# Later rotations and splits of q and k, side-by-side starts of the mixers' output products, and head transposes among the gates' products, in a four-layer block kernel

## The chip, the cores and the metric

The kernel runs on one core of one Trainium2 chip. The metric is device time in microseconds (us), the median of several executions; lower is better. Engines are called PE (TensorE, matmuls), ACT (ScalarE), DVE (VectorE), POOL (GpSimd) and SP (SyncE, which issues the DMAs).

## The reference

Two blocks of two layers each work on 256 latent tokens and 256 context tokens of 1024 features, in f32. Each layer is a mixer followed by an mlp (1024 to 4096 to 1024, squared relu); norms before both are modulated by numbers that come from a vector `c` through a matrix `w_mod` of 1024 x 6144. The first block's mixer has three branches, pooling, a gating unit and neighbourhood attention; its latent q and k are rotated. The second block's mixers are an mLSTM (both directions) and a windowed attention (SWA).

```python
def first_block(...):
    ...
        p, u, vs, q, k, v, gl = jnp.split(a @ w_in[l], SPLIT_POINTS, axis=-1)
        attn = neighbourhood_attention(apply_rope(to_heads(q), cos, sin), apply_rope(to_heads(k), cos, sin),
                                       to_heads(v), k_ctx, v_ctx, na_rpb[l], rows)
        mix = merge_branches(pool_mix(p, w_pool[l], pool_scale[l]), sgu_mix(u, vs, sgu_w[l], sgu_b[l]),
                             attn.reshape(h.shape[0], n_lat, NA_WIDTH), gl,
                             w_pool_out[l], w_sgu_out[l], w_attn_out[l], w_o[l])
        h = h + g1 * mix
        h = h + g2 * sq_relu_mlp(modulate(rms_norm(h, norm2_g[l]), sh2, sc2), w_ff1[l], w_ff2[l])
def merge_branches(pool_o, sgu_o, attn_o, gate_logits, w_po, w_so, w_ao, w_o):
    gp, gs, ga = jnp.split(jax.nn.sigmoid(gate_logits), N_BRANCH, axis=-1)
    y = gp * (pool_o @ w_po) + gs * (sgu_o @ w_so) + ga * (attn_o @ w_ao)
    return y @ w_o
```

In the mLSTM each head's result is normed over its 128 features, scaled by `head_norm`, multiplied by the sigmoid of an output gate (a product of the normed input) and then by `w_out`. In the SWA sixteen query heads share four key heads; latent q and k are rotated.

## The kernel before, in words

Features lie on the partitions, tokens along the free axis: 512 columns, context first (0 to 255), latents after (256 to 511). Every f32 operand is split into a high and a low f32r part. A large product goes by column tiles of 128 outputs (`gemm`, L204): a weight tile of 128 x 1024 comes by DMA into `raw`, ACT writes its high part `whi`, DVE (or POOL) the low part `wlo`, and for each of the eight row tiles PE issues three matmuls (high x high, high x low, low x high) into one PSUM bank. `raw`, `whi` and `wlo` have three slots each. A tile with both streams is 24 matmuls of 512 columns. With `head=n` the first n column tiles run side by side, one stream after the other (256 columns, SKEW row tiles apart), with `tail=n` the last n.

`evac` functions take a product up. They may return a part that `flush` issues when the next product's matmuls are under way (`take`, L196; `flush`, L233). `evac_k` (L813) and `evac_q` (L824) serve the first block's attention: they copy the latent half from PSUM to a T1 tile, split the context half straight from PSUM (`put_k`, L707; `put_q`, L714: ACT the high parts, DVE the low ones), rotate (`rope`, L687: a matmul with `perm`, a POOL and two DVE instructions) and split the rotated half. `gemm_rows` (L263) computes values with tokens on the partitions, four PSUM banks side by side, named by a list of tags. PSUM tags are mm (2 banks), mx, S (2), T (2) and acc. SBUF tags have fixed slots: A and B 16 each for the operands of large products in turn, Q 12, E 2, W 3, T1 9, G 2.

Modulation of later layers is worked off in pieces that `drip` (L470) issues after column tiles at a layer's rate (`RATES`); a piece is a DMA, an ACT scaling, a DVE accumulation and a POOL sum into `macc`. After a group of pieces PE sums over partitions (`acc`), ACT copies the sums (`mod_out`, L410), PE transposes them and DVE adds a bias; the transposition is put off by one flush. `need` (L481) issues all pending pieces that a use requires.

The attention output `evac_a` (L976, inside the loop over `wao`) gates a tile on DVE, adds the other branches on POOL (L979) and splits it. `gates_out` (L1229) computes the mLSTM's eight gate tiles; after them all, eight heads are transposed by PE into S banks, gated and split. The engines run their queues in order; a list scheduler orders each queue when the program is built, by priorities that follow the program order (`sooner`, L107, moves the taking up of a product ahead).

## Time and profile before

| | |
|---|---|
| median of 3 runs | 2331.84 us (2328.53 to 2334.13) |
| span of the profiled execution (no other time of it is given) | 2329.3 us |
| PE busy | 2228.5 us, 96% |
| DVE busy | 1620.0 us, 70% |
| ACT busy | 1148.6 us, 49% |
| POOL busy | 681.5 us, 29% |
| mean granted PE clock | 0.981 of full speed |

The span runs from the first to the last instruction. Busy shares are means over stages; a wait is read from the timeline of the engine that stood, where the bracket behind a row gives its idle time and what ended it. The granted clock is 1.00 at 2.4 GHz and 0.50 at 1.2 GHz. A line number can be that of a helper (L116 is `act`, L119 `stt`, L122 `mm`, L126 `tr`, L130 `split`), so tiles by tag say more. T stands for T1 tiles in SBUF and for the PSUM tag T.

### The profile page before, as it was taken

What the parts mean: (1) busy time and instruction counts of PE and PEld (TensorE: products, weight loads), DVE (VectorE), ACT (ScalarE), POOL (GpSimd) and SP (SyncE); (2) the same over time, 40 slices, a digit from 0 to 9 for tenths busy, and PEclk for the clock granted to TensorE, in tenths of its full rate; (3) what the DMA queues carried; (4) which work ended last, traced back from release to release, by engine and by line L of the source; (5) the groups of instructions that cost most, each with busy time, mean ns of one, the idle gap of its engine ahead of it and who ended that gap; (6) DMA issues with size and microseconds to landing.
All of it is one profiled execution on the core that took longest, in us unless ns stands there. A gap on an engine that the chain in (4) does not pass through costs nothing.

```text
span 2329.3 us, 36255 instructions
## 1 busy us (share of the span) xinstructions
PE 2228.5 (96%) x13402; PEld 1864.1 (80%) x13402; DVE 1620.0 (70%) x2762; ACT 1148.6 (49%) x2122; POOL 681.5 (29%) x530
## 2 busy tenths in 40 slices
PE   6899999999999999999999899999999999998998
PEld 3776777787777787798899867778777778768998
DVE  4876656677666885778877755678776566687766
ACT  3455434454443455655544645555443433665453
POOL 1540434524221542045300504154432222423001
PEclk9999999999999999999999999999999999999999
DMA  7351345445655443366554313254555532214552
GB/s 271 128 156 61 124 148 167 133 136 179 193 190 167 144 151 110 113 209 209 190 185 149 114 55 104 86 165 134 157 189 182 167 119 72 82 37 136 191 184 98
DMA packets 128145, 336.78 MB, mean 145 GB/s; under 512 B 14944, under 2 KB 24160, under 8 KB 127968
## 3 DMA queue, kind: packets, MB, share of 16 engines
q1 hardware_dynamic: 127968, 334.46, 44.5%
q8 instruction: 106, 1.74, 0.3%
q14 instruction: 71, 0.58, 0.1%
HBM read 333.36 MB, written 1.05 MB: 144 GB/s over the span
## 4 chain that ended last, share of the span: by engine, by line
PE 47%; DVE 6%; issue 2%; ACT 2%; POOL 2%; DMA 1%; DVEq 0%; POOLq 0%; SPq 0%; ACTq 0%
PE mm L122 27%; PE mx L122 11%; PE S L122 3%; PE num L122 2%; PE T L122 1%; PE pv L122 1%; PE T L126 1%; DVE wlo L130 1%; DMA mraw<-wmod_in 1%; DVE T L119 1%; DVE macc L119 1%; ACT whi L116 1%; POOL macc L449 1%; DVE A L119 1%; DVE B L119 0%
## 5 line engine op out<-in xcount | busy, mean ns | idle before, releaser
L122 PE MATMUL mm<-A,whi 128*128 128x256 f32 (+1 forms) x2600 | 666.2, 344 | 17.5 <-ACT A L116 7.6
L449 POOL TENSOR_TENSOR macc<-macc,mraw 128x512 f32<-128x512 f32 x244 | 363.3, 1489 | 697.0 <-ACT mraw L116 688.6
L122 PEld LDWEIGHTS mm<-A,whi 128*128 128x128 f32 x2600 | 446.7, 191 | 88.5 <-issue 18.8
L122 PE MATMUL mm<-B,whi 128*128 128x256 f32 (+1 forms) x1884 | 456.8, 333 | 8.4 <-DVE T L659 4.2
L122 PE MATMUL mm<-A,wlo 128*128 128x256 f32 (+1 forms) x1300 | 442.0, 340 | 0.0
L130 DVE TENSOR_TENSOR wlo<-raw,whi 128x1024 fp32r<-128x1024 f32 x252 | 344.7, 1370 | 136.4 <-ACT whi L116 134.8
L116 ACT ACTIVATE whi<-raw 128x1024 fp32r<-128x1024 f32 x273 | 287.6, 1055 | 280.7 <-PE mm L122 164.7
L122 PEld LDWEIGHTS mm<-B,whi 128*128 128x128 f32 x1884 | 319.2, 190 | 49.6 <-issue 11.1
L122 PE MATMUL mx<-A,whi 128*128 128x512 f32 (+1 forms) x1256 | 321.1, 343 | 1.6 <-ACT G L116 1.0
L116 ACT ACTIVATE mraw<-mraw,silu 128x512 f32<-128x512 f32 x244 | 175.2, 722 | 290.7 <-DVE macc L119 180.4
L122 PE MATMUL mm<-B,wlo 128*128 128x256 f32 (+1 forms) x942 | 312.1, 332 | 1.6 <-DVE wlo L130 1.6
L119 DVE SCALAR_TENSOR_TENSOR macc<-mraw,silu,macc 128x512 f32<-128x512 f32 x244 | 255.2, 1046 | 58.7 <-DMA mraw<-wmod_in 56.6
L122 PEld LDWEIGHTS mm<-A,wlo 128*128 128x128 f32 x1300 | 248.3, 191 | 28.4 <-issue 2.1
L116 ACT ACTIVATE whi<-Y 128x1024 fp32r<-128x1024 f32 x152 | 160.8, 1058 | 217.5 <-PE mm L122 145.8
L130 DVE TENSOR_TENSOR wlo<-Y,whi 128x1024 fp32r<-128x1024 f32 x148 | 192.4, 1300 | 92.2 <-ACT whi L116 92.0
L122 PEld LDWEIGHTS mx<-A,whi 128*128 128x128 f32 x1256 | 216.4, 190 | 32.0 <-issue 2.5
L122 PE MATMUL mx<-A,wlo 128*128 128x512 f32 (+1 forms) x628 | 214.9, 342 | 0.3 <-DVE wlo L130 0.3
L122 PE MATMUL mx<-B,whi 128*128 128x256 f32 (+1 forms) x836 | 201.4, 329 | 6.6 <-ACT B L116 3.3
L122 PEld LDWEIGHTS mm<-B,wlo 128*128 128x128 f32 x942 | 179.2, 190 | 21.0 <-issue 2.0
L509 POOL TENSOR_TENSOR sums<-sums,T 128x256 f32<-128x256 f32 x84 | 91.3, 1097 | 301.7 <-ACT T L116 300.2
L119 DVE SCALAR_TENSOR_TENSOR h<-mm,mod,h 128x256 f32<-128x256 f32 x278 | 125.8, 478 | 71.6 <-PE mm L122 71.3
L122 PEld LDWEIGHTS mx<-B,whi 128*128 128x128 f32 x836 | 140.9, 191 | 24.3 <-ACT B L116 3.9
(302 smaller groups left out, 3076.4 us busy)
## 6 DMA issues: line engine op xcount, KB each, us to landing
mraw<-wmod_in SPq DMA_DIRECT2D x352, 256.0 KB, 2.9
Y<-ff_in SPq DMA_DIRECT2D x152, 512.0 KB, 4.0
raw<-ff_in SPq DMA_DIRECT2D x104, 512.0 KB, 3.7
raw<-win_in SPq DMA_DIRECT2D x68, 512.0 KB, 3.6
raw<-mwin_in SPq DMA_DIRECT2D x17, 512.0 KB, 3.5
raw<-wo_in SPq DMA_DIRECT2D x16, 512.0 KB, 4.2
raw<-swin_in SPq DMA_DIRECT2D x10, 512.0 KB, 3.4
B<-wfirst_in SPq DMA_DIRECT2D x16, 256.0 KB, 5.4
```

Of the source, the lines that this page charges most:

```text
L116: return self.nc.scalar.activation(out, in_, func, **kw)
L119: return self.nc.vector.scalar_tensor_tensor(out, a, scalar, b, op0, op1)
L122: return self.nc.tensor.matmul(out, lhsT=lhsT, rhs=rhs, start=start, stop=stop, **kw)
L126: return self.nc.tensor.transpose(out, in_, self.ident[:k, :k])
L130: (eng or self.nc.vector).tensor_sub(lo, src, hi.bitcast(F32))
L449: self.nc.gpsimd.tensor_add(a1, a1, raw)
L509: (adder or self.nc.gpsimd).tensor_add(sums, sums, sq)
```

## The change

Eight parts. (1) The ACT copy of modulation sums is issued at once, their transposition two flushes later instead of one. (2) `evac_k` of the first block copies the whole PSUM bank once to an E tile; both halves are split in the put-off part. (3) `evac_q` copies the bank once to a W tile; rotation and splits are put off, with a flush after each `weigh`. (4) In `evac_a` DVE adds instead of POOL for the last two tiles. (5) The three output products `wo0`, `wo1` and `mwout` start with `head=3`; after such tiles there is no `drip`. (6) The mLSTM's and the SWA's `gemm_rows` use the S banks first. (7) Each mLSTM head's transposes, gating and split are put off behind the next gate product. (8) In the SWA k and q are copied once, rotated and split in put-off parts. The diff also strips comments and docstrings, which are left out below.

```diff
-            self.late.append(self.mod_out(i, (cg,), 4 * half, ps))
+            columns = self.mod_out(i, (cg,), 4 * half, ps)
+            self.late.append(lambda: self.late.append(columns))
...
-        self.flush()
+        while self.late:
+            self.flush()
...
     def evac_k(j, ps, a, e):
-        t = b.T1()
-        b.act(t, ps[:, L:])
-        b.put_k(kh[j], kl[j], slice(0, L), ps[:, :L])
+        t = b.t("E")
+        b.act(t, ps)
 
         def rest():
             k = b.T1()
-            b.rope(k, t, b.perm1, b.rope1)
+            b.rope(k, t[:, L:], b.perm1, b.rope1)
+            b.put_k(kh[j], kl[j], slice(0, L), t[:, :L])
             b.put_k(kh[j], kl[j], slice(L, T), k)
         return rest
 
     def evac_q(j, ps, a, e):
-        q, t, k = b.t("Y", (P, 2, T), F32R), b.T1(), b.T1()
-        b.act(t, ps[:, L - a:], scale=0.125)
-        if c0 == 0:
-            b.put_q(q, slice(0, L), ps[:, :L], 0.125)
-        b.rope(k, t, b.perm1, b.rope1)
-        b.put_q(q, slice(L, T), k)
+        q, t = b.t("Y", (P, 2, T), F32R), b.t("W")
+        b.act(t[:, a:], ps, scale=0.125)
         qs.append(q)
 
+        def rest():
+            k = b.T1()
+            b.rope(k, t[:, L:], b.perm1, b.rope1)
+            if c0 == 0:
+                b.put_q(q, slice(0, L), t[:, :L])
+            b.put_q(q, slice(L, T), k)
+        return rest
...
-    b.gemm([win[6 + j] for j in range(4)], xs, c0, evac_q)
+    b.gemm([win[6 + j] for j in range(4)], xs, c0, evac_q, flush=False)
...
             b.weigh(o, qt, pts, vt, vcols)
+            b.flush()
...
-            nc.gpsimd.tensor_add(t, t, y[d][:, c0:])
+            (nc.vector if d > 5 else nc.gpsimd).tensor_add(t, t, y[d][:, c0:])
...
-        b.gemm(aps, ys, c0, b.add_to_h(g1), tail=3, mid=b.norm(xs, LAT, A, S))
+        b.gemm(aps, ys, c0, b.add_to_h(g1), head=3, tail=3, mid=b.norm(xs, LAT, A, S))
...
-        b.gemm(aps, ys, c0, b.add_to_h(g1, then=scale), tail=3)
+        b.gemm(aps, ys, c0, b.add_to_h(g1, then=scale), head=3, tail=3)
...
-        b.gemm_rows([io["mwv"][hf, j] for j in range(4)], T, xs, ("mm", "mm", "S", "S"),
+        b.gemm_rows([io["mwv"][hf, j] for j in range(4)], T, xs, ("S", "S", "mm", "mm"),
...
-    def gates_out():
-        go = [b.t("B") for _ in range(8)]
-        b.gemm([win[16 + j] for j in range(8)], xs, 0,
-               lambda j, ps, a, e: b.act(go[j][:, a:e], ps, AF.Tanh, scale=0.5))
-        return go
+    def gates_out(hs):
+        ys = b.new_xs("A")
+        def evac(hd, ps, a, e):
+            go = b.t("B")
+            b.act(go, ps, AF.Tanh, scale=0.5)
+            def rest():
+                pt = b.ps("S")
+                for c in range(4):
+                    b.tr(pt[:, c * P:(c + 1) * P], hs[hd // 4][c][:, hd % 4, :])
+                t = b.t("E")
+                b.stt(t, go, 1.0, pt, ALU.add, ALU.mult)
+                b.act(ys[hd][0], t, scale=hn[:, hd:hd + 1])
+                b.stt(ys[hd][1], t, hn[:, hd:hd + 1], ys[hd][0].bitcast(F32),
+                      ALU.mult, ALU.subtract)
+            return rest
+        b.gemm([win[16 + j] for j in range(8)], xs, 0, evac)
+        return ys
 
     prj = project(0)
     hs = [heads(0, prj[0], prj[1], prj[3], states(0, prj[2], prj[3]))]
     prj = project(1)
     hs.append(heads(1, prj[0], prj[1], prj[3], states(1, prj[2], prj[3])))
-    go = gates_out()
-    ys = b.new_xs("A")
-    for hd in range(8):
-        pt = b.ps("S")
-        for c in range(4):
-            b.tr(pt[:, c * P:(c + 1) * P], hs[hd // 4][c][:, hd % 4, :])
-        t = b.t("E")
-        b.stt(t, go[hd], 1.0, pt, ALU.add, ALU.mult)
-        b.act(ys[hd][0], t, scale=hn[:, hd:hd + 1])
-        b.stt(ys[hd][1], t, hn[:, hd:hd + 1], ys[hd][0].bitcast(F32), ALU.mult, ALU.subtract)
+    ys = gates_out(hs)
...
-    b.gemm([io["mwout"][d] for d in range(8)], ys, 0, b.add_to_h(b.mod[i][:, 2]), tail=3,
+    b.gemm([io["mwout"][d] for d in range(8)], ys, 0, b.add_to_h(b.mod[i][:, 2]), head=3, tail=3,
            mid=b.norm(xs, LAT, A, S))
...
     def evac_k(j, ps, a, e):
-        if a < L:
-            b.put_k(kh[2 * j:2 * j + 2], kl[j], slice(0, L), ps[:, :L - a])
-        if e > L:
-            t, k = b.T1(), b.T1()
-            b.act(t, ps[:, max(L - a, 0):])
-
-            def rest():
+        t = b.T1()
+        b.act(t, ps)
+
+        def rest():
+            k = t
+            if a == L:
+                k = b.T1()
                 b.rope(k, t, perm2, rope2)
-                b.put_k(kh[2 * j:2 * j + 2], kl[j], slice(L, T), k)
-            return rest
-
-    def query(ps):
-        t, q = b.T1(), b.T1()
+            b.put_k(kh[2 * j:2 * j + 2], kl[j], slice(a, e), k)
+        return rest
+
+    def query(_, ps, a, e):
+        t, out = b.T1(), b.t("Q", (P, 2, L), F32R)
         b.act(t, ps, scale=0.125)
-        b.rope(q, t, perm2, rope2)
-        out = b.t("Q", (P, 2, L), F32R)
-        b.put_q(out, slice(0, L), q)
-        return out
+        qs.append(out)
+
+        def rest():
+            q = b.T1()
+            b.rope(q, t, perm2, rope2)
+            b.put_q(out, slice(0, L), q)
+        return rest
 
     b.gemm([win[8 + j] for j in range(2)], xs, 0, evac_k, head=2, pre=pre, flush=False)
-    b.gemm_rows([io["swv"][j] for j in range(2)], L, xs, ("mm", "mm", "mx", "S"),
+    b.gemm_rows([io["swv"][j] for j in range(2)], L, xs, ("S", "S", "mm", "mm"),
                 lambda c, ps: b.act(vt[c], ps))
     at = []
     qs = []
 
     def project(t):
-        b.gemm([win[t]], xs, L, lambda _, ps, a, e: qs.append(query(ps)))
+        b.gemm([win[t]], xs, L, query, flush=False)
...
             b.weigh(o, qt, pts, vt, vcols)
+            b.flush()
```

Three places in the order, names without their tile counters. First PE in the q products of the first mixer (`mm_1214`, `mx_1280` or `mx_1264`, `mm_1323` are banks of q tiles, `T_...<-...,perm` the rotation of the first q tile). Before:

```order
L122 MATMUL mm_1214<-A_113,wlo_1211 128x512
L122 MATMUL acc_1263<-macc,sel 32x128 x8
L122 MATMUL mx_1280<-A_99,whi_1276 128x512
L122 MATMUL mx_1280<-A_100,whi_1276 128x512
L122 MATMUL mx_1280<-A_99,wlo_1277 128x512
L122 MATMUL T_1247<-T_259_1240,perm_119_490 128x256
L122 MATMUL mx_1280<-A_101,whi_1276 128x512
```

Now:

```order
L122 MATMUL mx_1264<-A_113,whi_1260 128x512
L122 MATMUL mx_1264<-A_114,whi_1260 128x512
L122 MATMUL mx_1264<-A_113,wlo_1261 128x512
L122 MATMUL T_1290<-W_1240,perm_119_490 128x256
L122 MATMUL mm_1323<-A_99,whi_1319 128x512
L122 MATMUL mm_1323<-A_100,whi_1319 128x512
```

The rotation of the first q tile stood behind three matmuls of the second q tile; now it stands behind all 24.

Second, DVE at the start of the first mixer's output product (`G_3331`, `G_3332` are the last two gated tiles, `B_2937`, `B_2939` the low parts of row tiles 6 and 7 of its operand, `wlo_3538`/`wlo_3504` the second column tile's low weights, `wlo_3582`/`wlo_3510` the third's). Before:

```order
L130 TENSOR_TENSOR wlo_3538<-raw_3535,whi_3537 128x1024
L119 SCALAR_TENSOR_TENSOR macc<-mraw_3574,silu_71,macc 128x512
L119 SCALAR_TENSOR_TENSOR G_3331<-G_3331,mm_3431 128x512
L119 SCALAR_TENSOR_TENSOR macc<-mraw_3618,silu_71,macc 128x512
L130 TENSOR_TENSOR B_2937<-G_3331,B_2936 128x512
L119 SCALAR_TENSOR_TENSOR G_3332<-G_3332,mm_3448 128x512
L130 TENSOR_TENSOR wlo_3582<-raw_3579,whi_3581 128x1024
L130 TENSOR_TENSOR B_2939<-G_3332,B_2938 128x512
```

Now:

```order
L130 TENSOR_TENSOR wlo_3504<-raw_3501,whi_3503 128x1024
L119 SCALAR_TENSOR_TENSOR macc<-mraw_3766,silu_71,macc 128x512
L119 SCALAR_TENSOR_TENSOR G_3331<-G_3331,mm_3431 128x512
L119 SCALAR_TENSOR_TENSOR macc<-mraw_4005,silu_71,macc 128x512
L986 TENSOR_TENSOR G_3331<-G_3331,Y_2089 128x512
L119 SCALAR_TENSOR_TENSOR G_3332<-G_3332,mm_3448 128x512
L130 TENSOR_TENSOR B_2937<-G_3331,B_2936 128x512
L986 TENSOR_TENSOR G_3332<-G_3332,Y_2089 128x512
L130 TENSOR_TENSOR wlo_3510<-raw_3507,whi_3509 128x1024
L130 TENSOR_TENSOR B_2939<-G_3332,B_2938 128x512
```

The two sums (L986) stand on DVE, ahead of the third column tile's low weights, which on PE are now wanted 24 matmuls of 256 columns after the product's start; before, the third tile's were wanted after two whole tiles. On ACT the third tile's high part (`whi_3509`) stands between the splits of row tiles 6 and 7.

Third, PE at the values of the mLSTM's first half (`mm_13147` and `mm_13195` are the last q tile; the four banks of the values follow; every group is six matmuls). Before:

```order
L122 MATMUL mm_13147<-A_12547,wlo_13144 128x512
L122 MATMUL mm_13182<-whi_13188,A_12533 128x512
...
L122 MATMUL S_13184<-whi_13188,A_12533 128x512
...
L122 MATMUL mm_13183<-whi_13188,A_12533 128x512
...
L122 MATMUL S_13184<-whi_13188,A_12535 128x512
...
L122 MATMUL S_13185<-whi_13188,A_12533 128x512
```

Now:

```order
L122 MATMUL mm_13195<-A_12589,wlo_13192 128x512
L126 MATMUL T_13230<-ident_118,T_2559_13187 128x128
L122 MATMUL S_13237<-whi_13243,A_12575 128x512
...
L122 MATMUL S_13238<-whi_13243,A_12575 128x512
...
L122 MATMUL mm_13239<-whi_13243,A_12575 128x512
...
L122 MATMUL mm_13240<-whi_13243,A_12575 128x512
```

Both S banks come first, then the mm bank that the q tile before last has left, and last the one of the last q tile, `mm_13240`, which before was `mm_13183`, wanted after nine matmuls.

## Rows read from the trace of the kernel before

**Rows 1.** The page: busy us (share of the span) xinstructions.

```profile
PE 2228.5 (96%) x13402; PEld 1864.1 (80%) x13402; DVE 1620.0 (70%) x2762; ACT 1148.6 (49%) x2122; POOL 681.5 (29%) x530
```

**Rows 2.** Windows behind two waits: PE, PEld, DVE, ACT, POOL busy, PEclk, DMA, GB/s.

```profile
112.00:115.00 3.00, 3.00 (x9) 2.32 (x9) 3.00 (x3) 1.67 (x2) 1.44 (x1) 0.50 0.02 7
...
1345.00:1348.00 3.00, 3.00 (x8) 2.32 (x8) 2.31 (x6) 1.96 (x6) 0.00 (x0) 0.51 0.52 173
```

**Rows 3.** Timeline of PE (start us, us, what, xcount, [idle before <-releaser]), first mixer's third k tile.

```profile
111.66 0.47 PE L126 MATMUL T<-ident,T 128*128 128x128 f32 x1 [5.13 <-ACT T L116]
```

**Rows 4.** Timeline of ACT, the same place.

```profile
108.94 1.28 ACT L116 ACTIVATE Q<-T 64x256 fp32r<-64x256 f32 x3 [2.51 <-DVE T L694]
...
111.33 0.28 ACT L116 ACTIVATE T<-acc 128x128 f32<-128x128 f32 x1
```

**Rows 5.** Windows, columns as in rows 2: two stretches by VectorE's load.

```profile
100.00:125.00 25.00, 19.72 (x76) 15.32 (x77) 22.38 (x30) 14.75 (x30) 12.85 (x10) 0.86 0.27 91
...
1075.00:1100.00 25.00, 20.88 (x156) 20.30 (x155) 22.98 (x25) 14.02 (x25) 17.51 (x13) 0.91 0.72 225
```

**Rows 6.** Timeline of PE, the q tiles of the first mixer.

```profile
153.62 0.70 PE L122 MATMUL T<-T,perm 128*128 128x256 f32 x2 [2.17 <-ACT T L116]
162.45 0.70 PE L122 MATMUL T<-T,perm 128*128 128x256 f32 x2 [1.87 <-ACT T L116]
```

**Rows 7.** Timeline of PE without waits: 512 columns, then 256 columns.

```profile
103.88 0.39 PE L122 MATMUL mm<-A,wlo 128*128 128x512 f32 x1
104.11 0.40 PE L122 MATMUL mm<-A,whi 128*128 128x512 f32 x1
...
2003.01 0.28 PE L122 MATMUL mm<-B,wlo 128*128 128x256 f32 x1
2003.13 0.40 PE L122 MATMUL mm<-B,whi 128*128 128x256 f32 x2
```

**Rows 8.** Timeline of PE, second layer, start of the values.

```profile
896.68 0.47 PE L122 MATMUL mx<-whi,A 128*128 128x512 f32 x1 [3.24 <-DVE Q L712]
```

**Rows 9.** Timelines of PE and POOL, first mixer's output product.

```profile
406.17 0.63 PE L122 MATMUL mx<-B,whi 128*128 128x512 f32 x2
...
415.09 0.51 PE L122 MATMUL mx<-B,whi 128*128 128x512 f32 x1 [3.26 <-ACT B L116]
412.13 2.25 POOL L979 TENSOR_TENSOR G<-G,Y 128x512 f32<-128x512 f32 x1
```

**Rows 10.** Timelines of PE and ACT, mLSTM, first half's values.

```profile
1344.11 0.50 PE L122 MATMUL mm<-whi,A 128*128 128x512 f32 x1 [2.86 <-ACT Q L116]
1342.95 0.63 ACT L116 ACTIVATE nM<-W 64x512 fp32r<-64x512 f32 x1 [2.92 <-DVE W L1061]
```

**Rows 11.** What PE waited for (us in total, times, longest): 1525 to 1550, then 2000 to 2100.

```profile
PE mm L122 <- DVE A L119: 1.2, 2, 0.7
PE mm L122 <- ACT A L116: 0.5, 1, 0.5
...
PE S L122 <- ACT E L116: 1.9, 3, 1.4
PE S L122 <- DVE Q L119: 1.6, 1, 1.6
```

**Rows 12.** The page's groups: busy, mean ns of one, idle before.

```profile
L449 POOL TENSOR_TENSOR macc<-macc,mraw 128x512 f32<-128x512 f32 x244 | 363.3, 1489 | 697.0 <-ACT mraw L116 688.6
L119 DVE SCALAR_TENSOR_TENSOR macc<-mraw,silu,macc 128x512 f32<-128x512 f32 x244 | 255.2, 1046 | 58.7 <-DMA mraw<-wmod_in 56.6
```

**Rows 13.** Line 712 by tile: ns min/median/max, first and last start us.

```profile
L712 DVE TENSOR_TENSOR Q<-T,Q x20: 406/422/1469, 98.0 to 1992.0; 64x256 fp32r<-64x256 f32 x20
L712 DVE TENSOR_TENSOR Q<-mm,Q x12: 404/418/429, 92.9 to 1988.2; 64x256 fp32r<-64x256 f32 x12
```

**Rows 14.** What PE waited for, 1060 to 1120.

```profile
PE mm L122 <- DVE T L659: 4.2, 1, 4.2
PE T L122 <- POOL sums L509: 2.6, 1, 2.6
```

## The prediction

> **What bounds the kernel now.** I read the share of the span first [rows 1]: TensorE is busy for 2228.5 of 2329.3 us, VectorE for 1620.0, ScalarE for 1148.6. So TensorE sets the end, and a change that adds matmuls rather than removing them can win only out of the 100.8 us in which TensorE stands. The list of what it waited for, stretch by stretch, shows that these are single waits of 1 to 5 us, each at a hand-over from a product to ScalarE or VectorE. Third, the table of windows shows what a wait costs beside itself: five of the waits looked at here are followed by 3 us or more at the lower level of the granted clock (1.2 of 2.4 GHz; 0.50 and 0.51 in the first and the last of the five) [rows 2], with TensorE busy all the time; at half speed 3 us of work are 1.5 us lost. The timelines of PE, ACT, DVE and POOL around each wait then name the late instruction. The sum below is made against the profiled execution's span, 2329.3 us; the median of the three runs is 2331.84, and the 2.5 us between them are taken to stay.
>
> **The change part by part.**
>
> *Modulation transposes, first mixer.* TensorE stands 5.13 us at 111.66 for a transposition that waits for a ScalarE copy [rows 3]. That copy ran at 111.33, behind copies of k of which the first had waited 2.51 us for VectorE [rows 4]. Now it stands ahead of those and its transposition one product later. At most 5.1 + 1.5 (clock) = 6.6 us go. But VectorE is busy for 22.38 of 25 us here [rows 5]; the low parts of the next weights come from it in order, and a product without waits would soon reach weights that are not ready. What is late next is a wlo. Bounds 0 and 6.6; I take 2.5, nearer to the lower end since 90% of that stretch is VectorE's.
>
> *Rotations of q, first mixer.* The rotation matmul stands three matmuls into the next product and waits 2.17 and 1.87 us for a ScalarE copy [rows 6]. In the new order it stands behind all 24 matmuls of that product, 24 x 0.23 = 5.5 us later (0.23 from the starts of 512-column matmuls) [rows 7]. Both waits go, and with the second one a half-clock stretch: 2.17 + 1.87 + 1.5 = 5.5. Between 0 and 5.5 I take 5, as the cover is over twice the wait. The bank of the product itself is now read by one copy instead of several.
>
> *k in the second layer.* The product of values stands 3.24 us for a bank whose last reader is a subtraction on VectorE that followed a rotation's sum and two of ScalarE's copies [rows 8]. One ScalarE copy now frees it, and the low parts come from the copy. 3.24 + 1.5 for the clock = 4.7, between none and that; the copy is one instruction that waits for the product alone, so I take 4.5.
>
> *Output product, first mixer.* TensorE stands 3.26 us for the last row tile of its operand: ScalarE's split waited for a GpSimd sum of 2.25 us queued behind two modulation sums [rows 9]. Now VectorE adds the last two, and the first three column tiles run side by side, so that the last row tile is wanted later. Removed: 3.3 + 1.5 = 4.8. But the third tile's weights are now wanted 24 matmuls of 256 columns, 24 x 0.12 = 2.9 us [rows 7], after the start at 406.17 [rows 9], so at 409.1. Their slot is free only after the product that ends there. In the new order the way to them then is a gating, a modulation sum, the sum, the split of row tile 6 and the high part; at about 1 us for each (1.05 for the modulation sum of the same 512 columns [rows 12]) the high part is there at 411.2 and the low part, 1 us more, at 412.2: an estimated new wait of 3 us. I take a gain of 2, between none and 4.8.
>
> *Values of the mLSTM.* TensorE waits 2.86 us until 1344.11 for a bank that ScalarE has to copy out, because ScalarE's queue stood for 2.92 us on a VectorE scan ahead of that copy [rows 10]. The scan and that order stay. Nine matmuls had run, so the product began at 1344.11 - 2.86 - 9 x 0.23 = 1339.2. Now twelve matmuls into two S banks and six into a free one come first: 1339.2 + 18 x 0.23 = 1343.3, which leaves 0.8 us of wait. Gain 2.0, and 1.5 if the clock then stays up: between 1 and 3.5, I take 3.
>
> *Heads' transposes among the gates' products.* TensorE waited 1.2 + 0.5 = 1.7 us for the operand in 1525 to 1550 [rows 11]. The operand's slots (tag A, 16) are those of the gates' own operand, so the splits still can't be written before the last gate product has read them; only transposes and the first gatings move forward. I take 1.5, with 0 and 1.7 as the bounds.
>
> *SWA.* Its waits are 1.9 + 1.6 us in 2000 to 2100 [rows 11]. Rotation and split of q(t+1) now come after the weighing of tile t, so that only the next project product lies between them and the scores that need them, while ScalarE and VectorE are busy with softmax there. A gain of 2, bounds -3 (a loss, as much as is now waited) and 3.5.
>
> *What is added.* Six column tiles (three here, three of the mLSTM) are issued as 48 matmuls of 256 instead of 24 of 512: 24 x (2 x 0.12 - 0.23) = 0.24 us each, 1.4 in all. The second layer's output product was 256 wide already. Skipping the drip for three tiles moves 3 x 1.4, 3 x 0.7 and 3 x 1.4 modulation pieces, ten in all, into the mlp that follows; a piece is 1.05 us of VectorE and 1.49 of GpSimd [rows 12]. Most lie beside products that have time for them; I charge 1.6 us. DMAs of these pieces move along with them, their number stays.
>
> The subtractions of k's context half read SBUF twice now, not PSUM and SBUF. There are 20 of them (4 tiles, 2 halves, 2 layers, and 4 in the SWA). In the trace those that read PSUM last 404 to 429 ns, and those that read SBUF twice have nearly the same median, 422, but reach 1469 [rows 13]. If each of the 20 were stretched so, VectorE would have 20 x 1.05 = 21 us more; the median says most are not, and I charge nothing. The Trainium skill has a rule that speaks against this step: "GPSIMD Engine Reference", section Specifications, says that GpSimd shares its SBUF interfaces with VectorE and contends with VectorE instructions that have two SBUF inputs. The rows agree as to which group has the long ones; by the rule alone the subtractions next to GpSimd's rotations would all be long, and the sum would be nearer to the second rival below.
>
> Sum: -2.5 - 5 - 4.5 - 2 - 3 - 1.5 - 2 + 1.4 + 1.6 = **-17.5 us**, so a span of 2311.8 and a median of **2314 us**.
>
> **The rivals.**
>
> *Everything pays.* All waits named go with their half clocks: 6.6 + 5.5 + 4.7 + 4.8 + 3.5 + 1.7 + 3.5 = 30.3, less the 1.4 of split matmuls: 2303. For it: these waits are single hand-overs, with products on either side of each. Against it: the 22.38 of 25 us, and the third weights.
>
> *VectorE takes over.* Where TensorE no longer waits for a hand-over it waits for low parts of weights. Then the first, fourth, sixth and seventh parts give nothing, the q part half, the mLSTM part 1.5, and the added 3.0 stay: -2.5 - 4.5 - 1.5 + 3.0 = -5.5, 2326. For it: VectorE's 22.38 of 25 us at 100 and 22.98 of 25 at 1075 [rows 5]; against it: 70% over the span.
>
> *Slower: modulation pieces displaced into the norms.* The ten pieces come due around the norm at the mlp's start. There TensorE already stands 4.2 us for VectorE's modulated norm and 2.6 for GpSimd's sums of squares in 1086 to 1120 [rows 14]. Were each piece in line with the norm, it would delay it by 1.05 + 1.49 = 2.5 us, 25 in all and 23 more than charged: 2314 + 23 = 2337. It decides against the change from about eight pieces in line. Against it: TensorE works on context tiles beside most of a norm, and after the first and third mixer the pieces are spread at 2.0 and 1.8 a tile.
>
> *It doesn't do what it says.* The order rows show the moves in place, so this gets no chance of its own.
>
> **How the numbers follow.** Forecast 0.52, everything pays 0.14, VectorE takes over 0.20, slower 0.14. About 0.2%, 4.7 us, is what a measurement of this kernel can tell from no change: below 2327.2 counts as faster, above 2336.5 as slower. The second rival lies at that lower edge and is split, 0.09 faster and 0.11 same. Faster 0.52 + 0.14 + 0.09 = 0.75, same 0.11, slower 0.14. The forecast's own range is 2306 to 2323 (its unknown bounds); for 8 in 10 it reaches down to 2299, 4 us past the case in which everything pays, and up to 2334, which takes in the second rival and leaves out the slower one.
>
> **What would show it.** Right: no T wait on ACT T at the second k tile and at the q tiles of the first mixer; no wait for DVE Q before the second layer's values; the stretches behind them at full clock; a first wait of about 3 us on whi or wlo in the first output product; under 1 us at the mLSTM's values. Wrong: waits on wlo in the stretch after 112 that add up to what went; waits for DVE T or POOL sums at the mlp starts of over 10 us more; SWA longer than its part now. If the half-clock stretches stay though the waits go, the five terms of 1.5 fall out and the gain is up to 7 us smaller.

## The result, and the profile after

The change made the kernel slower: 2350.75 us (median, 2347.44 to 2358.72) beside 2330.48 of the kernel before on the same chip, ratio 1.0091 with a 95% interval of 1.007 to 1.0112. Forecast were 2314 us and a range of 2299 to 2334. The profiled execution has a span of 2345.5 us where before had 2329.3, 16.2 more. The page of the kernel after, busy times as in [rows 1]:

```profile
PE 2239.2 (95%) x13546; PEld 1880.7 (80%) x13546; DVE 1610.4 (69%) x2766; ACT 1156.7 (49%) x2124; POOL 658.3 (28%) x526
```

TensorE has 144 matmuls more, as forecast (six tiles of 48 instead of 24), and is busy for 10.7 us more, of which these explain 1.4; the mean granted clock is 0.975 where before had 0.981. So only 5.5 of the 16.2 us are more standing (106.3 us for 100.8): most of the loss is the same work taking longer, as it did in the half-clock stretches behind waits [rows 2]. No other engine is closer to full than before. What TensorE waits for, the places of [rows 3], [rows 6], [rows 8 to 10] and of the SWA tell in the timeline of PE in the kernel after (the bracket is the wait before the row):

```profile
113.83 0.67 PE L122 MATMUL T<-E,perm 128*128 128x256 f32 x2 [3.73 <-DVE T L695]
...
172.18 1.52 PE L122 MATMUL S<-Q,Y 128*128 128x512 f32 x2 [6.81 <-ACT E L116]
...
411.39 0.51 PE L122 MATMUL mm<-B,whi 128*128 128x256 f32 x2 [1.94 <-ACT whi L116]
...
413.19 0.39 PE L122 MATMUL mm<-B,wlo 128*128 128x256 f32 x1 [1.18 <-DVE wlo L130]
...
895.47 0.50 PE L122 MATMUL mx<-whi,A 128*128 128x512 f32 x1 [2.33 <-ACT E L116]
...
1338.55 0.50 PE L122 MATMUL mm<-whi,A 128*128 128x512 f32 x1 [0.57 <-ACT Q L116]
...
2019.86 2.24 PE L122 MATMUL S<-Q,Q 128*128 128x512 f32 x3 [3.13 <-DVE Q L119]
```

Each named wait is gone or shorter, but most have a successor: 5.13 us for ScalarE's copy became 3.73 for VectorE's half of a rotation; the two waits of 2.17 and 1.87 at the q tiles became one of 6.81 for a softmax; 3.24 at the values became 2.33; the SWA's 1.6 for VectorE's split became 3.13, while its 1.9 for ScalarE [rows 11] is gone. Only the mLSTM's values went as hoped, from 2.86 to 0.57. And one place is new, the norm at the start of the mLSTM's mlp:

```profile
1594.69 0.39 PE L122 MATMUL mm<-B,wlo 128*128 128x256 f32 x1 [2.58 <-DVE wlo L130]
...
1603.29 0.65 PE L122 MATMUL acc<-macc,sel 128*32 128x128 f32 x8 [4.38 <-DVE macc L119]
1605.73 0.65 PE L122 MATMUL acc<-macc,sel 128*32 128x128 f32 x8 [1.79 <-POOL macc L449]
...
1607.05 0.43 PE L122 MATMUL T<-mean,sums 128*128 128x1 f32 x2
...
1610.24 1.22 PE L122 MATMUL T<-ident,sm 128*128 128x128 f32 x4 [1.49 <-POOL sm L524]
1613.00 0.58 PE L122 MATMUL mx<-B,whi 128*128 128x256 f32 x1 [1.54 <-ACT B L116]
```

There TensorE waits for the last modulation sums (`acc<-macc`), and the norm's own first product (`T<-mean,sums`) stands behind them.

To see the stages apart I take marks that every version has: the `T<-mean,sums` that begins a norm (a: first layer's mlp, b: second layer's mixer, c: mLSTM's mixer, f: mLSTM's mlp, g: SWA; of two streams the second, in c the first) and the first `kv` product of each half of the mLSTM (d, e). The table has their starts in the timeline of PE, as the kernel's own minus before's; h is the span. Before: a 463.99, b 842.97, c 1279.58, d 1368.86, e 1450.46, f 1595.31, g 1971.10, h 2329.3 us. The experiments are told below.

| kernel | a | b | c | d | e | f | g | h |
|---|---|---|---|---|---|---|---|---|
| the change | -3.2 | 0.2 | -7.7 | -9.3 | -5.5 | **11.7** | 11.5 | 16.2 |
| e1_drip | 5.4 | 5.5 | 12.6 | 9.6 | 8.8 | 11.0 | 11.5 | 11.8 |
| e2_mwout_plain | 3.5 | 6.4 | -2.0 | -5.1 | -1.3 | 15.3 | 15.8 | 18.4 |
| e3_banks | 1.9 | 5.5 | -3.7 | -5.5 | 0.8 | 17.6 | 17.7 | 19.9 |
| e4_swa_old | 1.9 | 5.9 | 1.4 | -0.7 | 1.7 | 21.5 | 21.4 | 22.4 |
| e5_l1mlp | 0.5 | 4.4 | 6.4 | 4.9 | 5.1 | **2.0** | 2.4 | 3.7 |
| e6_q_old | -3.9 | -0.3 | -10.5 | -12.2 | -8.4 | 13.8 | 13.2 | 16.7 |
| e8_mod_old | 1.2 | 5.2 | 1.3 | 1.3 | 5.1 | 19.5 | 19.6 | 29.3 |
| e9_mix_mlp | -5.4 | -1.8 | -2.0 | -3.3 | -3.2 | -7.9 | -7.8 | -6.6 |
| e7_best | -2.2 | -2.8 | 8.3 | 8.5 | 8.8 | 8.9 | 7.8 | 6.8 |
| e10_mix_att | -4.8 | -3.2 | -8.8 | -11.7 | -9.1 | -13.8 | -13.6 | -14.0 |
| e12_q_new | 1.9 | 4.3 | 1.9 | -1.5 | 2.7 | -0.9 | 1.0 | -0.2 |
| e11_before_rate | 0.4 | -0.2 | 12.1 | 5.9 | 6.0 | 6.5 | 6.2 | 8.0 |
| e13_handovers | -5.5 | -6.2 | -6.8 | -9.9 | -10.7 | -12.2 | -11.5 | -12.5 |
| e14_products | -1.7 | 0.3 | -1.5 | 0.8 | 6.4 | 8.5 | 8.8 | 11.2 |

At d the change is ahead by 9.3 us. Then it loses 3.8 to e, 17.2 from e to f, and 4.7 in the SWA stage (g to h). These are single profiles, and the same code differs in them by up to 9 us at c (the change and e2 to e4, which are one program up to there) and by 10 at f (the change and e4). So verdicts below go by the timed ratios, and by the marks only for the length of one stretch where it jumps.

**What moved to f.** The pieces of modulation work can be counted: VectorE's instructions that read `mraw`, stretch by stretch (windows; VectorE busy and count, clock, DMA). Before:

```profile
0.00:464.00 464.00, 77.64 (x72) 0.97 0.46 149
464.00:843.00 379.00, 71.31 (x80) 1.00 0.51 161
843.00:1096.00 253.00, 32.27 (x32) 0.99 0.52 167
1096.00:1280.00 184.00, 0.00 (x0) 0.96 0.53 172
1280.00:1450.00 170.00, 15.46 (x16) 0.96 0.28 89
1450.00:1579.00 129.00, 22.99 (x24) 1.00 0.40 129
1579.00:1607.00 28.00, 1.97 (x3) 0.88 0.33 104
```

After:

```profile
0.00:464.00 464.00, 66.51 (x65) 0.98 0.45 145
464.00:843.00 379.00, 78.99 (x88) 1.00 0.52 166
843.00:1096.00 253.00, 25.81 (x24) 0.97 0.50 163
1096.00:1280.00 184.00, 0.00 (x0) 0.97 0.53 172
1280.00:1450.00 170.00, 23.65 (x24) 0.95 0.30 97
1450.00:1579.00 129.00, 16.80 (x16) 0.96 0.36 115
1579.00:1607.00 28.00, 7.66 (x9) 0.86 0.40 125
```

The first layer's mlp catches up what its mixer skipped (88 for 80). The second layer's mixer gives 24 instead of 32, and its mlp, whose rate is 0, catches up none; the mLSTM's first half takes these eight over (24 for 16), and nine pieces stand in the last window. As f comes 11.7 us later in the change, the windows at one time are not the same place there; the 16 us just ahead of each kernel's own f are (before, after):

```profile
1579.30:1595.30 16.00, 0.00 (x0) 0.79 0.21 65
...
1591.00:1607.00 16.00, 4.95 (x6) 0.76 0.48 148
```

Before has none there; in the change six stand directly ahead of the norm's first product, which has to wait for their sums.

### The profile page after: what moved, and what is told of

Same layout as the page of the kernel before. It is cut to its first block, busy times and chain, and to the rows that moved or that the text cites. A ratio compares the mean times of both kernels' runs of the same rounds, so it can differ in the third digit from the quotient of the medians.

```text
span 2345.5 us, 36521 instructions
## 1 busy us (share of the span) xinstructions
PE 2239.2 (95%) x13546; PEld 1880.7 (80%) x13546; DVE 1610.4 (69%) x2766; ACT 1156.7 (49%) x2124; POOL 658.3 (28%) x526
## 4 chain that ended last, share of the span: by engine, by line
PE 49%; DVE 4%; issue 2%; POOL 2%; ACT 2%; DMA 1%; DVEq 0%; POOLq 0%; ACTq 0%
PE mm L122 29%; PE mx L122 12%; PE S L122 2%; PE num L122 2%; PE pv L122 1%; PE T L122 1%; PE T L126 1%; DVE macc L119 1%; DVE wlo L130 1%; DVE T L119 1%; POOL macc L449 0%; DMA mraw<-wmod_in 0%; PE kv L122 0%; ACT whi L116 0%; DVE A L119 0%
## 5 line engine op out<-in xcount | busy, mean ns | idle before, releaser
L449 POOL TENSOR_TENSOR macc<-macc,mraw 128x512 f32<-128x512 f32 x244 | 353.6, 1449 | 716.5 <-ACT mraw L116 699.5
L122 PE MATMUL mm<-B,whi 128*128 128x256 f32 (+1 forms) x1916 | 463.6, 332 | 7.5 <-DVE h L119 2.5
L130 DVE TENSOR_TENSOR wlo<-raw,whi 128x1024 fp32r<-128x1024 f32 x252 | 335.6, 1333 | 143.7 <-ACT whi L116 141.9
L122 PEld LDWEIGHTS mm<-B,whi 128*128 128x128 f32 x1916 | 326.1, 192 | 47.1 <-issue 4.8
L122 PE MATMUL mx<-A,whi 128*128 128x256 f32 (+1 forms) x1272 | 325.6, 343 | 0.0
L122 PE MATMUL mm<-B,wlo 128*128 128x256 f32 (+1 forms) x958 | 317.4, 331 | 8.6 <-DVE wlo L130 7.2
L122 PE MATMUL mx<-A,wlo 128*128 128x256 f32 (+1 forms) x636 | 216.5, 340 | 0.0
L122 PEld LDWEIGHTS mm<-B,wlo 128*128 128x128 f32 x958 | 183.9, 192 | 27.8 <-DVE wlo L130 8.5
L511 POOL TENSOR_TENSOR sums<-sums,T 128x256 f32<-128x256 f32 x84 | 85.7, 1028 | 325.7 <-ACT T L116 324.2
```

What stands on the lines that cost most here:

```text
L122: return self.nc.tensor.matmul(out, lhsT=lhsT, rhs=rhs, start=start, stop=stop, **kw)
L130: (eng or self.nc.vector).tensor_sub(lo, src, hi.bitcast(F32))
L449: self.nc.gpsimd.tensor_add(a1, a1, raw)
L511: (adder or self.nc.gpsimd).tensor_add(sums, sums, sq)
```

## The experiments

**Is it the displaced pieces?** Theory A: tiles that skip their share leave a group over, and it comes due in front of the norm at f. Rival: the hand-overs themselves made new waits. e1 gives the shares of the side-by-side tiles after all, e2 takes only the mLSTM's own product back, e5 gives pieces in the second layer's mlp.

```diff
# e1_drip: gemm(..., drips=False); drips=True at the three products with head=3
-            if m == 1:
+            for _ in range(m if m == 1 or drips else 0):
                 self.drip()
# e2_mwout_plain
-    b.gemm([io["mwout"][d] for d in range(8)], ys, 0, b.add_to_h(b.mod[i][:, 2]), head=3, tail=3,
+    b.gemm([io["mwout"][d] for d in range(8)], ys, 0, b.add_to_h(b.mod[i][:, 2]), tail=3,
# e5_l1mlp
-RATES = ((1.4, 2.0), (0.7, 0.0), (1.4, 1.8), (0.0, 0.0))
+RATES = ((1.4, 2.0), (0.7, 0.3), (1.4, 1.8), (0.0, 0.0))
```

> The changed kernel, except that each of the three side-by-side tiles of the output products again gives its share of modulation work (as one tile did before). Theory A (the modulation group that the skipped shares push to the start of the mlp after the mLSTM makes TensorE stand there for its sums): the wait of 4.4 us for VectorE's accumulation and the half-clock stretch behind it go, the stretch from the mLSTM's output product to the fourth tile of its mlp is 10 to 14 us shorter than in the changed kernel, total near 2338. Rival B (the third tile's weights and the three tiles side by side themselves cost it): that stretch keeps its length, total near 2350. Side effect by A: the second layer's output product gives back part of the 7.7 us that it gained.

> The changed kernel with the mLSTM's output product begun tile by tile as before (no side-by-side start there, and so its modulation shares as before). Theory A: the stretch behind it is 10 to 14 us shorter, total near 2338, the wait for VectorE's accumulation gone. Theory B: the same. Against e1 it tells the start itself from the skipped shares: if e1 and e2 agree within 2 us in that stretch the start itself is worth nothing, if e1 is shorter by 3 us or more the start pays once the shares are given.

> The changed kernel with one number changed: the second layer's mlp works off 0.3 modulation pieces a column tile instead of none, so that the group which the skipped shares of that layer's output product push into the mLSTM is done before it. Theory A (that displaced group costs 9 us in the mLSTM's second half and 13 us at the start of its mlp): both losses go, the second layer's output product keeps its gain of 7 to 8 us, and the kernel is 15 to 22 us faster than the changed one, near 2331, equal to the kernel before. Rival (the second half's waits and the stand at the mlp's start come from the order of the banks and the gates' transposes): no more than 5 us faster, near 2347.

e1: 2343.01 us, ratio 1.005 (1.0032 to 1.0069), 0.41% or 9.6 us faster than the change, but not the 2338 expected. From e to f it loses 2.2 where the change lost 17.2: the long wait is gone. But it loses 7.1 from b to c, in the second layer, where the change gains 7.9; at that layer's mlp start TensorE now stands for GpSimd's sums of squares, 5.2 us where before had 2.6 [rows 14]:

```profile
PE T L122 <- POOL sums L511: 5.2, 1, 5.2
```

So pieces that now come directly ahead of that norm cost there, by the marks, about what they save later. e2: 2350.61, ratio 1.0087 (1.0062 to 1.0113), no different from the change where Theory A had 2338, and e to f still loses 16.6: the group that comes late is left over from the second layer, not from the mLSTM's own product. e5: 2337.05, ratio 1.0028 (1.0013 to 1.0043). From e to f it gains 3.1; in its trace the norm's product at f starts at 1597.29 (1607.05 in the change). But the second layer's output product doesn't keep its gain as I had expected: b to c is 2.0 longer than before's, where the change was 7.9 shorter. On balance the one number in `RATES` is worth 14 us of the 20.

**Single parts taken back.**

```diff
# e3_banks: the mLSTM's values as before
-        b.gemm_rows([io["mwv"][hf, j] for j in range(4)], T, xs, ("S", "S", "mm", "mm"),
+        b.gemm_rows([io["mwv"][hf, j] for j in range(4)], T, xs, ("mm", "mm", "S", "S"),
# e4_swa_old: the SWA's key, query and tags as before (gist)
-    b.gemm_rows([io["swv"][j] for j in range(2)], L, xs, ("S", "S", "mm", "mm"),
+    b.gemm_rows([io["swv"][j] for j in range(2)], L, xs, ("mm", "mm", "mx", "S"),
-        b.gemm([win[t]], xs, L, query, flush=False)
+        b.gemm([win[t]], xs, L, lambda _, ps, a, e: qs.append(query(ps)))
# e6_q_old: evac_q of before, and no flush behind weigh
-    b.gemm([win[6 + j] for j in range(4)], xs, c0, evac_q, flush=False)
+    b.gemm([win[6 + j] for j in range(4)], xs, c0, evac_q)
# e8_mod_old
-            columns = self.mod_out(i, (cg,), 4 * half, ps)
-            self.late.append(lambda: self.late.append(columns))
+            self.late.append(self.mod_out(i, (cg,), 4 * half, ps))
```

> The changed kernel with the mLSTM's values again in the order mm, mm, S, S of banks. Theory (the S-first order frees the first half's wait but puts the two late bank copies behind ScalarE's modulation scalings in the second half): the first half's wait of about 2.9 us comes back near 1335, and in the second half the waits of 1.7 us for ScalarE's state copy with 10 us at half clock go, 5 to 8 us; net 2 to 5 us faster than the changed kernel. Rival (those waits come from where the modulation pieces fall, whatever the banks): the second half keeps its 7 us and the kernel is 3 to 4 us slower than the changed one.

> The changed kernel with the SWA's part as before (k from PSUM, rotation of q right behind its product, bank order as before). If the later rotation costs the SWA (its stage is 3 us longer in the changed kernel, with a new wait of 3.1 us for VectorE's split before the first scores and 6.8 us at half clock): 2 to 6 us faster than the changed kernel, that wait gone, the two half-microsecond waits for VectorE before the values back. If its length comes from what stands before it: no difference beyond 1 us.

> The changed kernel with the first block's q taken up as before (rotation behind the next product's first matmuls, splits straight from PSUM, no flush behind the weighing). Theory C (the put-off rotations fall into the first attention, where the scores of the second query tile then wait 6.8 us for ScalarE and 7 to 14 us run at half clock): the two rotation waits of about 2 us come back, the 6.8 us go, and the stretch from 100 to 300 us is 3 to 6 us shorter than in the changed kernel; the second layer's attention stage 2 to 4 us shorter too; total near 2343. Rival (the wait comes from the k part or from the modulation copies): the 6.8 us wait stays and the two rotation waits come on top, 3 to 5 us slower.

> The changed kernel with the modulation sums taken up as before (ScalarE's copy and the transposition both one flush later). If the new place of the copy is what removed the 5.1 us wait in the first mixer: that wait comes back, 4 to 7 us slower around 110 us, little elsewhere. If the single copy of k removed it (ScalarE's queue is no longer behind VectorE there): no wait comes back and the kernel is within 2 us of the changed one.

e3: 2353.41, ratio 1.0096 (1.0074 to 1.0118); the second half's loss (d to e, 6.3) stays, so the S banks don't cause it, and the wait at the first half's values is back:

```profile
1338.71 0.51 PE L122 MATMUL mm<-whi,A 128*128 128x512 f32 x1 [2.67 <-ACT Q L116]
```

e4: 2352.62, ratio 1.0086 (1.0061 to 1.0111), total not to be told from the change; its SWA stage (g to h) is 1.0 us longer than before's, the change's 4.7; but e1 and e5, with the change's SWA, have 0.3 and 1.3. e6: 2348.26, ratio 1.0062 (1.0043 to 1.0081): 0.29% or 6.8 us better than the change by the ratios, 2.5 by the medians, and the intervals overlap. Its waits are as Theory C had them: the 6.81 us in front of the scores are gone, and the two rotation waits are back:

```profile
151.05 0.48 PE L122 MATMUL T<-T,perm 128*128 128x256 f32 x1 [2.03 <-ACT T L116]
...
159.76 0.48 PE L122 MATMUL T<-T,perm 128*128 128x256 f32 x1 [0.54 <-ACT T L116]
```

e8: 2359.66, ratio 1.0112 (1.008 to 1.0144): 0.2% slower than the change by the ratios, with intervals that overlap, so it isn't shown that the transposes' part is worth keeping. At the third k tile the 5.13 us for ScalarE do not come back without it:

```profile
108.24 0.30 PE L126 MATMUL T<-ident,T 128*128 128x128 f32 x1 [1.61 <-DVE T L694]
...
116.02 0.45 PE L122 MATMUL T<-E,perm 128*128 128x256 f32 x1 [1.91 <-DVE mod L422]
```

That is 3.52 us for VectorE, beside 3.73 in the change. So about the wait the rival was right: it goes without the earlier copy of the sums, and of the parts that are left only k's single copy lies at this place. With so much lost at f, these runs can't size a part; a mixture without that loss can.

**Mixtures.** All have q and the SWA as before. e9 gives 0.3 pieces a tile in the second layer's mlp, e10 instead 0.9 for 0.7 in its mixer, e7 is e9 with shares also given at the first layer's and the mLSTM's side-by-side tiles.

```diff
-RATES = ((1.4, 2.0), (0.7, 0.0), (1.4, 1.8), (0.0, 0.0))
+RATES = ((1.4, 2.0), (0.7, 0.3), (1.4, 1.8), (0.0, 0.0))
# e10_mix_att, e11_before_rate, e12_q_new, e14_products:
+RATES = ((1.4, 2.0), (0.9, 0.0), (1.4, 1.8), (0.0, 0.0))
```

> The change with three edits together: the q part and the sliding-window part as before, and 0.3 modulation pieces per share in the second layer's mlp, where the change gives none. Theory (the losses are separate and add): the run with the mlp rate alone stood at 2337; the q part put back took 2.5 us off (2350.8 to 2348.3), and the sliding-window stage was 3.0 to 3.6 us shorter with its old part: 2331, and within 2328 to 2334. Rival (what is gained in one stage is given back in the next, through half-clock stretches or late pieces): 2336 to 2341, no better than the mlp rate alone.

> As the other mixture, but the pieces come back in the second layer's attention products (0.9 a share instead of 0.7) and none in its mlp. Theory (what costs is only that a group of eight pieces is left over for the second half of the mLSTM and the norm behind it; where it stands ahead of that makes little difference): one group more ahead of the second layer's output product, no stand at the mLSTM's mlp, 2329 to 2336. Rival (a group in the attention's products stands in front of the score tiles and is paid there): the second layer's attention is 5 us or more longer than in the change and the total 2338 or more.

> As the mixture with 0.3 pieces per share in the second layer's mlp, and the side-by-side tiles of the first layer's and the mLSTM's output product give their three shares each, the second layer's do not. Theory: the shares at the first layer's product cost what the run with all shares lost there (some 4 us at the end of that stage against the change), and give it back as fewer pieces further on: 2328 to 2336. Rival (pieces inside a side-by-side block always cost their own wait, as at the second layer's product): 2336 to 2342, worse than the mixture by 5 or more.

e9: 2325.98, ratio 0.9976 (0.9965 to 0.9987). e10: 2320.03, ratio 0.9966 (0.9954 to 0.9978), both faster than expected, and f holds its lead (-13.8). In e10 the second layer's mixer has its 32 pieces again (same view as above, by this kernel's own marks):

```profile
840.00:1091.00 251.00, 34.71 (x32) 0.97 0.51 169
```

e7: 2341.78, ratio 1.005 (1.0037 to 1.0064), 16 us behind e9. The rival had the size, but its reason isn't shown: of the 16.8 us that e7 is behind at f, 11.3 arise from b to c, in the second layer, whose side-by-side tiles give no shares in either kernel. There TensorE waits for GpSimd's sums of squares as it does in e1:

```profile
1092.45 0.37 PE L122 MATMUL T<-mean,sums 128*128 128x1 f32 x1 [5.20 <-POOL sums L511]
```

In the 15 us ahead of this product e1 and e7 have four pieces, before three (and a wait of 2.6), e9, e10 and the change none (and no such wait). As at f, the pieces cost where they come directly ahead of a norm, and no share inside a side-by-side block is needed for that.

**Controls on e10.** e11 is the kernel before with e10's rate alone; e12 is e10 with the change's q part (edits as named).

> The kernel before with 0.9 pieces per share in the second layer's attention in place of 0.7, and nothing else: the control of the mixture that measured 0.9966 of before. There the kernel before has no group left over in front of the mLSTM's mlp, so by my theory (the rate only repairs what skipped shares displaced) it gains nothing: 2326 to 2336, ratio 0.998 to 1.003. Rival (the mixture owes its gain to the rate, not to the parts of the change): 2318 to 2325, ratio 0.995 to 0.9975.

> The mixture with the attention rate of 0.9, but with the q part of the change put back in (rotations and splits of q behind the next product). If the q part costs what taking it out gave at 0.7 (2.5 us in the times, 3.3 us at the end of the first layer's attention, by the wait for a column of scores and the half clock behind it): 2321 to 2327, with a wait of the score tile of some 7 us before the first layer's scores. My prediction's term (the q part gains 5 us at first layer, waits of TensorE replaced by nothing): 2315 to 2318.

e11: 2337.86, ratio 1.0032 (1.0019 to 1.0045). The rate alone is a loss, not e10's gain; I had expected no change and missed by 2 us, since eight pieces too early cost as well (40 pieces for 32 between b and c; 12 us at c, half of them back at d). e12: 2332.64, ratio 1.0013 (1.0001 to 1.0024), 0.47% or 11 us over e10: the q part loses, by more than I expected. In these two profiles 6.7 of that are there at a, 10.7 at c. The wait is the change's at 172.18:

```profile
172.06 1.52 PE L122 MATMUL S<-Q,Y 128*128 128x512 f32 x2 [6.79 <-ACT E L116]
```

VectorE's queue in e12 just before shows why (timeline of DVE; the first scores are finished by 160.4, where the next product's matmuls begin):

```profile
160.76 1.85 DVE L119 SCALAR_TENSOR_TENSOR Y<-W,Y 64x256 fp32r<-64x256 f32 x2
162.64 0.87 DVE L119 SCALAR_TENSOR_TENSOR Y<-T,Y 64x256 fp32r<-64x256 f32 x2
163.54 0.75 DVE L119 SCALAR_TENSOR_TENSOR macc<-mraw,silu,macc 128x512 f32<-128x512 f32 x1
164.21 0.42 DVE L695 TENSOR_TENSOR T<-T,rope 128x256 f32<-128x256 f32 x1
166.08 1.51 DVE L130 TENSOR_TENSOR wlo<-raw,whi 128x1024 fp32r<-128x1024 f32 x1 [1.45 <-ACT whi L116]
167.51 0.94 DVE L696 TENSOR_TENSOR T<-T,T 128x256 f32<-128x256 f32 x1
168.38 0.41 DVE L732 TENSOR_REDUCE sm<-S 128x1 f32<-128x256 f32 x1
```

The scores' first reader (L732, the softmax's maximum) is at VectorE 8 us after them, behind rotations and splits of q tiles, which now are put off to just here, a modulation sum and the low parts of a weight. Until it has run, ScalarE has no exponential, and the second pair of scores no bank. In e10 the same reader follows its scores at once (167.37, scores at 166.51), with the old wait of 2.15 in front of a rotation:

```profile
167.37 0.42 DVE L732 TENSOR_REDUCE sm<-S 128x1 f32<-128x256 f32 x1 [1.69 <-PE S L122]
...
159.99 0.82 PE L122 MATMUL T<-T,perm 128*128 128x256 f32 x2 [2.15 <-ACT T L116]
```

**What is left: hand-overs or products?** e13 is e10 without the side-by-side products (`head=3` taken out at all three, rate 0.7 again); e14 is the kernel before with only these products, the two sums on VectorE, and the rate 0.9.

> The mixture of the attention rate 0.9 without its products: all three output products begin as before, every tile gives its share, the rate is 0.7 again. What is left of the change are the hand-overs: modulation transposes, k, the sums on VectorE for two tiles, S banks first, heads' transposes. My prediction's terms for these (2.5 + 4.5 + 3 + 1.5 = 11.5) give 2319; the stage readings of the change (3.6 at the first attention, some 3 at k, 4 at the mLSTM's first half, 5 at the gates, less what is given back) 2316 to 2322. Rival (the mixture owes its gain to the side-by-side products and the better placed pieces, the hand-overs only shift waits): 2326 to 2331.

> The kernel before with only the side-by-side starts of the three output products, the sums on VectorE for two tiles, and the attention rate 0.9. By my theory the skipped shares are only moved (the gain of some 8 us at the second layer's product is what the displaced pieces cost elsewhere): 2326 to 2332. Rival (the products themselves are the gain): 2318 to 2323. If this and the run of the hand-overs add up to the mixture's -8 us (ratio 0.9966), the parts are independent.

e13: **2319.51 us**, ratio 0.9947 (0.9936 to 0.9959), where the prediction's terms gave 2319; that they fit so well is in part luck, as single terms do not (below). e14: 2337.86, ratio 1.003 (1.0019 to 1.0041), against both theories: the products lose 7 us with the rate that they need, and the gain of the second layer's (b to c: 1.8 here, 5.6 in e10, 0.6 in e13) is given back in the mLSTM (7.9 from c to e). Added up the two make -12.4 + 7.0 = -5.4, and e10 measured -7.9; the 2.5 us between lie inside the intervals, and the two sums on VectorE stand in both, so it stays open whether the parts are independent. The lowest is e13, faster than before by 0.5% and than the change by 1.4% (its interval just touches e10's):

```profile
PE 2224.7 (96%) x13402; PEld 1861.3 (80%) x13402; DVE 1631.7 (70%) x2766; ACT 1151.4 (50%) x2122; POOL 677.8 (29%) x526
```

TensorE's busy time is 3.8 us below before's with the same 13402 matmuls, at a mean granted clock of 0.982 for 0.981. VectorE has 11.7 more; the four sums moved over from GpSimd (median 0.55 us) are a small part of that.

## Why the prediction was wrong, step by step

By ratios the way from before to the change is a ladder: hand-overs -0.53% (e13), products with the rate 0.9 +0.19 (e10), q part +0.47 (e12), old rate and the SWA part +0.78 (the change, +0.91). Times 2330 us: -12.4, +4.4, +11.0, +18.2; of the last, e5 shows 14.7 (1.0091 to 1.0028) to be displaced pieces, and some 3.5 remain for the SWA and for what the parts do to each other. The first rung has an interval of 0.12% either way; the others are differences of two ratios and have 0.17 to 0.24 (4 to 6 us). So the hand-overs' gain, the q part's loss and the displaced pieces are clear of noise; the products' 4.4 is barely so, and the 3.5 are not.

- **Modulation transposes, first mixer** (forecast -2.5): the cause was wrong. The wait shrank from 5.13 to 3.73 us, but in e8 it does so without the transposes' part, by k's single copy; that this part gains anything is not shown. "What is late next is a wlo" was wrong too: it is VectorE's half of the rotation, 3.73 us. In e13 transposes, k and the sums on VectorE together have a at -5.5.
- **Rotations of q** (forecast -5): the step that failed outright, by 16 us (+11.0 by e12 against e10). I asked whether the rotation's operand would be ready ("the cover is over twice the wait"; the cover is 21 matmuls and not 24, as the rotation stood behind three already), and it is; I did not ask what the put-off part is queued ahead of on VectorE. It is the softmax.
- **k, second layer** (forecast -4.5): mis-sized. The wait went from 3.24 to 2.44 in e13, 888.97 for 896.68: -7.7 at that product where b had -6.2, so 1.5 us. The copy doesn't wait "for the product alone": ScalarE's queue brings the wait back, as `ACT E`. That the subtractions cost nothing held for TensorE as far as the rows show: none of the waits above ends with one. VectorE pays 4.1 us, as the 16 that read the copy last 10.9 us in all, 16 x 0.423 = 6.8 at their median. e13's wait, and this line's subtractions in the change:

```profile
888.97 0.79 PE L122 MATMUL mx<-whi,A 128*128 128x512 f32 x1 [2.44 <-ACT E L116]
...
L714 DVE TENSOR_TENSOR Q<-T,Q x24: 406/422/950, 95.0 to 2004.6; 64x256 fp32r<-64x256 f32 x24
L714 DVE TENSOR_TENSOR Q<-E,Q x16: 402/423/1520, 91.2 to 897.4; 64x256 fp32r<-64x256 f32 x16
```

  They have the median of before's [rows 13], and single ones last up to 1520 ns. The Trainium skill's rule of shared interfaces ("GPSIMD Engine Reference", Specifications) agrees with these rows and [rows 13] in that only instructions with two SBUF inputs have such outliers, but it made no sum here. The traces of before and of the change also show when: each of these subtractions that lasts over 0.9 us starts while a GpSimd instruction is under way. Before has both kinds beside one GpSimd sum, the one from PSUM at 0.41 us, the one from SBUF, which starts while it runs, at 1.20:

```profile
119.88 0.41 DVE L712 TENSOR_TENSOR Q<-mm,Q 64x256 fp32r<-64x256 f32 x1
120.22 1.20 DVE L712 TENSOR_TENSOR Q<-T,Q 64x256 fp32r<-64x256 f32 x1
...
119.85 1.29 POOL L449 TENSOR_TENSOR macc<-macc,mraw 128x512 f32<-128x512 f32 x1 [0.97 <-ACT mraw L116]
```

- **Output product, first mixer** (forecast -2): the working was right, the wait for the third tile's weights is 1.94 + 1.18 = 3.12 us where 3 was estimated. But in e13, with the sums on VectorE and no side-by-side tiles, the 3.26 us shrink to three waits of 0.48, 0.53 and 0.57 (1.58 together), half of what the tiles bring with them, and a stands at -5.5 for e10's -4.8: the sums gain, the tiles add nothing.
- **mLSTM's values** (forecast -3): right in the mechanism. 0.57 us of wait are left where 0.8 were reckoned, and e3, with the old banks, has 2.67 again. In the medians e3 is 2.7 us slower than the change (1.2 by the ratios), which fits, but the intervals overlap.
- **Heads' transposes** (forecast -1.5): e to f gains 1.5 in e13, as forecast, but between single profiles and with other moves in that stretch; it isn't shown by a run of its own.
- **SWA** (forecast -2): no gain. The stage (g to h) is 0.3 to 9.7 us longer than before's in the seven profiles with the new part (the change, e1, e2, e3, e5, e6, e8), and -1.2 to 2.4 in the eight others. That leans to a loss of some 3 us, but the ranges overlap and no timed run has this part alone, so it isn't settled. The first scores wait 3.13 us for VectorE's split of q, where before waited 1.6 there and 1.9 for ScalarE [rows 11].
- **What is added** (1.6 for ten pieces, "into the mlp that follows"): this failed next, by 13.1 us (14.7 measured for 1.6). A skipped share is made up only where the rate leaves room: in the first layer's mlp it was, in the second's, whose rate is 0, it was not, and eight pieces came through the mLSTM to the norm at f. The slower rival had the mechanism; its price was 2.5 us a piece, measured are 14.7 / 8 = 1.8 (with its interval, 1.1 to 2.6). It put the place at the mlp that follows, and had 0.14 of the chance. Had I counted pieces per stage in the order of the changed kernel, its chance would have been the larger.

The rival in which everything pays is out, and the one in which VectorE takes over was half right: at the q tiles VectorE decided, not through weights but through its queue's order.

## What to carry to other kernels

When work is put off so that TensorE need not wait for it, look at what stands behind its new place on the engine that executes it: here the softmax did. When a change skips shares of background work, follow the backlog to the point that demands it, through every stage, and reckon with stages that give nothing; one rate decided 14 us, and what cost were the pieces that came directly ahead of a norm. And test parts of a bundle apart: five hand-overs of this one are worth 12 us together (how much each of the five, no run tells), and the rest took 33 away.

## What the runs showed of the hardware that was not expected

The granted clock after the same wait differed between executions. In the change, TensorE stood 6.81 us up to 172.18, and 4 us later the clock was full (windows; PE, PEld, DVE, ACT, POOL busy, PEclk):

```profile
172.00:176.00 4.00, 3.82 (x10) 2.29 (x10) 1.83 (x8) 1.17 (x5) 0.00 (x0) 0.52 0.58 198
176.00:180.00 4.00, 4.00 (x28) 2.77 (x28) 1.03 (x3) 2.60 (x5) 0.00 (x0) 1.00 0.00 0
```

In e4, with the same instructions there and a wait of 6.96 us up to 172.07, it was not:

```profile
172.00:176.00 4.00, 3.93 (x10) 2.32 (x10) 1.72 (x8) 1.17 (x4) 0.00 (x0) 0.50 0.54 183
176.00:180.00 4.00, 4.00 (x13) 2.17 (x14) 0.40 (x1) 0.82 (x2) 0.00 (x0) 0.50 0.00 0
```

So TensorE worked at the lower level for at least 4 us longer after the same wait, which is some 2 us of work lost; part of the spread in the table's column a is the clock, not the code. Why the one stretch is longer stays open.
